# Start addresses of matmul operands: activation tiles and high weight parts at different 32-byte slots of a 512-byte line

## The chip, the cores and the metric

The kernel runs on one core of a Trainium2 chip. The metric is the device time of one execution in microseconds, lower is better. Activations are 256 tokens wide; all weights come from HBM once per use.

## The reference

One layer of a hybrid decoder (`SEQ` 256, `D_MODEL` 2048, 16 heads of 128, `D_FF` 5632), in float32:

```python
h = rmsnorm(x, g_mix)
proj = h @ w_in                      # q, k, v of 16 heads, then three gates
o_a = stick_breaking_attention(...)  # 4 heads
o_b = moba_attention(...)            # 6 heads
o_c = dilated_attention(...)         # 6 heads
merged = (gates[:, :, 0] * (flat(o_a) @ w_branch[:ea])
          + gates[:, :, 1] * (flat(o_b) @ w_branch[ea:eb])
          + gates[:, :, 2] * (flat(o_c) @ w_branch[eb:]))
x = x + merged @ w_out
h2 = rmsnorm(x, g_ffn)
gu = h2 @ w_gu
x = x + (silu(gu[..., :D_FF]) * gu[..., D_FF:]) @ w_down
```

## The kernel before

Nearly all work is the product of 256 tokens with a weight matrix. Tokens are taken as two halves of 128 (`t`), the depth in pieces of 128 rows (`k`), the output in columns of `NB` = 512. Each factor is kept as two tiles of type float32r, a high part and a low part. `split` (L102) makes them: ScalarE (ACT in the profile) casts the source to the high part (L103), VectorE (DVE) subtracts it from the source and writes the low part (L104). `product` (L157) adds three matmuls into one PSUM bank:

```python
nc.tensor.matmul(ps, ah, wh, start=start, stop=False, **how)   # L159
nc.tensor.matmul(ps, ah, wl, start=False, stop=False, **how)   # L160
nc.tensor.matmul(ps, al, wh, start=False, stop=stop, **how)    # L161
```

The first operand (`ah`, `al`: 128x128 of an activation) is what TensorE (PE) loads beforehand with a LDWEIGHTS (PEld in the profile); the second (`wh`, `wl`: 128x512 of a weight part) is streamed through the array. So in the profile's words the model's weights are streamed and the model's activations are loaded.

Weights: `weights` (L106) and `load` (L275) fetch two depth pieces at a time, 512 KB, with SyncE's (SP) queue into `w_raw` (4 buffers) or, where a sum is wanted first, `g_raw`. `weights` and `parts` (L281) split them into `w_hi` and `w_lo`, five buffers each, all in one pool, `wpool` (L82), at the right end of the memory. `project` (L139) is a plain product. `project_pair` (L315) and `down_pair` (L842) trade some of the products for sums of tiles: VectorE adds quarters of the weights into `u` or `g_raw` (L300, L311), and sums of activations are kept as further pairs of parts.

Activations: `Columns` (L185) holds a pair for the whole depth: `h` for the first projections, `o` for the branch projections, `m` for the output projection. `Chunks` (L235) holds a pair for each 512 rows of depth, and for some of them four more tiles: `h2` for the feed-forward part, `a` for the down projection. `Sums` and `Both` (L209, L265) hold the pairs of sums (`b_shi`, `b_slo` and the like). They are allocated in pools at the left end of the memory (`p1`, `pe`, `h2p`, `pd`), `m` at the right end.

The stages follow one another: first projections with the attention woven in (10 to 552 us of the profiled span), branch projections (to 644), output projection (to 734.5), feed-forward (to 1197), down projection. Attention's own matmuls and the transposes (L181) are fp32. A scheduler orders the instructions of each engine when the program is built; DMAs and a few instructions are kept in the order written. A tile's address follows from the order and the sizes of the allocations in its pool alone.

Of the kernel before, what the change touches and what calls it, by code (L numbers as in the profile page):

```python
# [10 lines left out]
F32 = mybir.dt.float32  # L11
F32R = mybir.dt.float32r
# [6 lines left out]
P = 128  # L19
D = 2048  # L20
S = 256
# [8 lines left out]
NB = 512  # L30
# [25 lines left out]
def hybrid_block(ctx: ExitStack, tc: tile.TileContext, x, g_mix, w_in, q_gain, k_gain, w_branch, w_out,  # L56
# [5 lines left out]
    consts = ctx.enter_context(tc.tile_pool(name="consts", bufs=1))  # L62
# [4 lines left out]
    att = pat.enter_context(tc.tile_pool(name="att", bufs=1, space=PSUM))  # L67
    dram = ctx.enter_context(tc.tile_pool(name="dram", bufs=1, space=DRAM))

    gmix = consts.tile([KT, P], F32, name="gmix")  # L70
    nc.scalar.dma_start(gmix, g_mix[0].rearrange("(k p) -> k p", p=P))
    nc.scalar.preload_act_table_set("natural_log_exp_and_others")
# [5 lines left out]
    def pool(stack, name, side, bufs=1):  # L78
        return stack.enter_context(tc.tile_pool(name=name, bufs=bufs, side=side, reuse_waits="tile"))

    h2_stack, ph1, pm, pgx = ExitStack(), ExitStack(), ExitStack(), ExitStack()
    wpool = pool(ctx, "wpool", "right", 5)  # L82
    scratch = pool(ctx, "scratch", "right", 12)
    gx = pool(pgx, "gx", "right", 2)
# [17 lines left out]
    def split(hi, lo, src):  # L102
        nc.scalar.copy(hi, src)  # L103
        nc.vector.tensor_sub(lo, src, hi.bitcast(F32))  # L104

    def weights(w, row0, nk, col0, fine):  # L106

        for c in range(0, nk, 2):
            raw = wpool.tile([P, 2, NB], F32, name="w_raw", bufs=4)
            hi = wpool.tile([P, 2, NB], F32R, name="w_hi")  # L110
            lo = wpool.tile([P, 2, NB], F32R, name="w_lo")
            src = w[row0 + c * P: row0 + (c + 2) * P, col0: col0 + NB].rearrange("(k p) n -> p k n", p=P)
            if fine and c < 4:
                for k in range(2):
                    nc.scalar.dma_start(raw[:, k, :], src[:, k, :])
                    split(hi[:, k, :], lo[:, k, :], raw[:, k, :])
                    yield c + k, hi[:, k, :], lo[:, k, :]
                continue
            nc.sync.dma_start(raw, src)
            split(hi, lo, raw)  # L120
            for k in range(2):
                yield c + k, hi[:, k, :], lo[:, k, :]
# [4 lines left out]
    def advance(queue):  # L127
        while queue:
            try:
                next(queue[0])  # L130
                return
            except StopIteration:
                queue.pop(0)
# [5 lines left out]
    def project(acts, k0, w, row0, nk, col0, fine=False, last=1):  # L139


        ps = banks()
        held = []
        for k, w_hi, w_lo in weights(w, row0, nk, col0, fine):
            if k:
                advance(stages)
            if k % 2 == 0 and k:
                advance(slow_stages)
            held.append((k, w_hi, w_lo))
            if k < nk - last or k == nk - 1:  # L150
                for t in range(NT):
                    for kk, hi, lo in held:
                        product(ps[t], *acts.plain(t, k0 + kk), hi, lo, kk == 0, kk == nk - 1)
                held = []
        return ps
# [26 lines left out]
        return pt  # L182


    class Columns:  # L185


        def __init__(self, pl, name, nk):
            self.hi, self.lo = (pl.tile([P, nk, S], F32R, name=f"{name}_{n}") for n in ("hi", "lo"))

        def put(self, c, t, src):
            k, q = slice(4 * c, 4 * c + 4), slice(t * P, (t + 1) * P)
# [16 lines left out]
    class Sums:  # L209
# [6 lines left out]
                    self.place(pl, c)  # L216

        def place(self, pl, c):
            self.s[c] = [pl.tile([P, 4, S], F32R, name=f"{self.name}_s{n}{c}") for n in ("hi", "lo")]

        def put_sums(self, c, t0, t1, whole=None):
            sums(t0, t1)
# [12 lines left out]
    class Chunks(Sums):  # L235
# [9 lines left out]
        def place(self, pl, c):  # L245
            if c in self.wc:
                super().place(pl, c)
                self.t[c] = [[pl.tile(sh, F32R, name=f"{self.name}_{t}{n}{c}") for n in ("hi", "lo")]
                             for t, sh in enumerate(([P, 4, P], [P, 2, P]))]
            else:  # L250
                self.t[c] = [pl.tile([P, 4, S], F32R, name=f"{self.name}_{n}{c}") for n in ("hi", "lo")]

        def put(self, c, t, src):
            if c in self.wc:
# [24 lines left out]
        return raw  # L279

    def parts(src):  # L281
        hi = wpool.tile([P, 2, NB], F32R, name="w_hi")
        lo = wpool.tile([P, 2, NB], F32R, name="w_lo")
        split(hi, lo, src)
        advance(stages)
        split_count[0] += 1
        if split_count[0] % 2:
            advance(slow_stages)
        return hi, lo
# [15 lines left out]
    def begin_pair(acts, w, colA, colB):  # L305

        b11, b12 = (quarter(acts, w, 0, col0) for col0 in (colA, colB))
        p11 = [parts(b) for b in b11]
        u = [gx.tile([P, 2, NB], F32, name="u") for _ in acts.wc]
        for a, b, d in zip(b11, b12, u):  # L310
            nc.vector.tensor_add(d, a, b)  # L311
        b21 = quarter(acts, w, 1, colA)
        return p11, b12, u, b21, [parts(b) for b in b21]

    def project_pair(acts, w, colA, colB, begun=None, nxt=None):  # L315
# [7 lines left out]
        def form(ps, f, srcs, start, stop, split=False):  # L323
            for i, c in enumerate(acts.wc):
                wh, wl = srcs[i] if split else parts(srcs[i])
                for j in range(2):
                    product(ps, *acts.form(f, c, j), wh[:, j], wl[:, j], start and i + j == 0,
                            stop and i + j == len(acts.wc))
# [417 lines left out]


    pe = pool(ctx, "pe", "left")
    h2 = Chunks(pool(h2_stack, "h2p", "left"), "h", KT // 4, WC)

    def next_h(c, xc):
# [215 lines left out]
```

## Time and profile before

| | |
|---|---|
| median of the runs | 1434.8 us (1433.98 and 1435.62) |
| profiled execution, its own time | 1435.5 us |
| its span | 1433.8 us |
| granted TensorE clock | 0.998 |
| PE busy | 1422.4 us (99%), 6407 matmuls |
| PE weight loads busy | 1173.4 us (82%) |
| VectorE busy | 1195.9 us (83%) |
| ScalarE busy | 880.0 us (61%) |
| DMA | 310.09 MB, mean 216 GB/s |

A matmul's duration in the profile is longer than the distance to the next one, since matmuls overlap; the distance of their starts, the pitch, is what adds up to the span. A row of the view by windows gives the stretch, its length, and for each engine busy time and, in brackets, how many instructions touch the stretch; then the clock, the DMA share and GB/s.

### The profile page before, as it was taken

The page shows a single profiled execution, that of the slowest core. Times are in us where ns is not written, and L with a number is a line of the kernel's source. Part 1 is how long each engine was busy: PE and PEld are TensorE (multiplying, and loading weights), DVE is VectorE, ACT ScalarE, POOL GpSimd, SP SyncE. Part 2 cuts the span into 40 slices and gives each one's busy share as a digit, 9 for nine tenths or more (in the row PEclk, how much of TensorE's full clock was granted, in tenths as well). Part 3 has the DMA queues.
Part 4 walks back from the last instruction along what each step waited for, and adds up shares of the span by engine and source line. Part 5 has one row for each costly group of instructions (what it writes and reads, how often), then busy time and mean ns, then how long its engine had stood idle before and what let it go on. Part 6 is the DMA issues. An engine that isn't in the chain of part 4 may idle for free. (4 is left out here: it accounts for less than half of the span.)

```text
span 1433.8 us, 17776 instructions
## 1 busy us (share of the span) xinstructions
PE 1422.4 (99%) x6407; PEld 1173.4 (82%) x6407; DVE 1195.9 (83%) x1263; ACT 880.0 (61%) x1131; POOL 72.6 (5%) x133
## 2 busy tenths in 40 slices
PE   9999999999999999999999999999999999999998
PEld 7888888888888888888887888888888888888887
DVE  7798797966999887776689999999999998886775
ACT  6567866766766665444556666666666666654453
POOL 1000000000000002100100000000000010100000
PEclk9999999999999999999999999999999999999999
DMA  8763647465656768866686667566666766767553
GB/s 267 253 224 113 233 117 250 118 219 179 219 194 247 245 203 282 287 218 216 217 298 222 216 209 262 201 228 231 222 203 200 243 205 223 262 229 242 188 170 97
DMA packets 154472, 310.09 MB, mean 216 GB/s; under 512 B 10672, under 2 KB 12288, under 8 KB 154384
## 3 DMA queue, kind: packets, MB, share of 16 engines
q1 hardware_dynamic: 142624, 274.24, 57.1%
q0 software_dynamic: 10000, 32.62, 6.9%
q10 hardware_dynamic: 1760, 2.11, 0.4%
q8 instruction: 50, 0.82, 0.2%
q14 instruction: 38, 0.31, 0.1%
HBM read 292.65 MB, written 16.27 MB: 215 GB/s over the span
## 5 line engine op out<-in xcount | busy, mean ns | idle before, releaser
L104 DVE TENSOR_TENSOR w_lo<-w_raw,w_hi 128x1024 fp32r<-128x1024 f32 (+1 forms) x338 | 408.7, 1215 | 94.6 <-ACT w_hi L103 90.7
L103 ACT CAST w_hi<-w_raw 128x1024 fp32r<-128x1024 f32 (+1 forms) x338 | 351.5, 1047 | 176.3 <-PE qs L161 65.8
L103 ACT CAST w_hi<-g_raw 128x1024 fp32r<-128x1024 f32 x184 | 192.5, 1053 | 122.5 <-PE ps L161 39.5
L104 DVE TENSOR_TENSOR w_lo<-g_raw,w_hi 128x1024 fp32r<-128x1024 f32 x184 | 219.6, 1222 | 35.6 <-ACT w_hi L103 34.9
L103 ACT CAST w_hi<-u 128x1024 fp32r<-128x1024 f32 x138 | 145.0, 1053 | 134.9 <-DVE u L300 64.8
L104 DVE TENSOR_TENSOR w_lo<-u,w_hi 128x1024 fp32r<-128x1024 f32 x138 | 166.5, 1222 | 36.2 <-ACT w_hi L103 34.8
L160 PE MATMUL ps<-w_lo,h_hi 128*128 128x512 f32 x368 | 144.1, 392 | 0.0
L161 PE MATMUL ps<-w_hi,h_lo 128*128 128x512 f32 x368 | 143.0, 390 | 0.0
L159 PE MATMUL ps<-w_hi,h_hi 128*128 128x512 f32 x368 | 140.4, 393 | 0.0
L160 PE MATMUL qs<-w_lo,h_hi 128*128 128x512 f32 x332 | 129.9, 391 | 0.8 <-DVE w_lo L104 0.8
L161 PE MATMUL qs<-w_hi,h_lo 128*128 128x512 f32 x332 | 129.4, 390 | 0.0
L159 PE MATMUL qs<-w_hi,h_hi 128*128 128x512 f32 x332 | 126.2, 391 | 0.0
L300 DVE TENSOR_TENSOR u<-u,g_raw 128x1024 f32<-128x1024 f32 x80 | 94.4, 1219 | 0.0
L159 PEld LDWEIGHTS ps<-w_hi,h_hi 128*128 128x128 f32 x368 | 69.2, 188 | 15.1 <-ACT h_hi L103 1.1
L161 PEld LDWEIGHTS ps<-w_hi,h_lo 128*128 128x128 f32 x368 | 69.3, 188 | 14.2
L160 PEld LDWEIGHTS ps<-w_lo,h_hi 128*128 128x128 f32 x368 | 69.3, 188 | 14.0
L160 PEld LDWEIGHTS qs<-w_lo,h_hi 128*128 128x128 f32 x332 | 62.3, 188 | 13.9 <-DVE w_lo L104 1.2
L161 PEld LDWEIGHTS qs<-w_hi,h_lo 128*128 128x128 f32 x332 | 62.4, 188 | 12.8
L159 PEld LDWEIGHTS qs<-w_hi,h_hi 128*128 128x128 f32 x332 | 62.3, 188 | 12.7
L311 DVE TENSOR_TENSOR u<-g_raw 128x1024 f32<-128x1024 f32 x40 | 48.8, 1221 | 23.3 <-DMA g_raw<-in_w_in 18.0
L159 PE MATMUL v<-w_hi,h_hi 128*128 128x512 f32 x120 | 47.5, 396 | 0.2 <-ACT w_hi L103 0.2
L160 PE MATMUL v<-w_lo,h_hi 128*128 128x512 f32 x120 | 47.1, 392 | 0.0
(376 smaller groups left out, 2915.4 us busy)
## 6 DMA issues: line engine op xcount, KB each, us to landing
w_raw<-in_w_in SPq DMA_DIRECT2D x118, 512.0 KB, 4.7
g_raw<-in_w_gu SPq DMA_DIRECT2D x88, 512.0 KB, 5.3
w_raw<-in_w_gu SPq DMA_DIRECT2D x88, 512.0 KB, 6.4
g_raw<-in_w_in SPq DMA_DIRECT2D x72, 512.0 KB, 5.8
w_raw<-in_w_down SPq DMA_DIRECT2D x64, 512.0 KB, 4.6
w_raw<-in_w_branch SPq DMA_DIRECT2D x32, 512.0 KB, 5.0
w_raw<-in_w_out SPq DMA_DIRECT2D x32, 512.0 KB, 4.7
g_raw<-in_w_down SPq DMA_DIRECT2D x24, 512.0 KB, 5.2
```

What stands on the lines that cost most here:

```text
L103: nc.scalar.copy(hi, src)
L104: nc.vector.tensor_sub(lo, src, hi.bitcast(F32))
L159: nc.tensor.matmul(ps, ah, wh, start=start, stop=False, **how)
L160: nc.tensor.matmul(ps, ah, wl, start=False, stop=False, **how)
L161: nc.tensor.matmul(ps, al, wh, start=False, stop=stop, **how)
L300: tc.keep_in_program_order(nc.vector.tensor_add(d, d, a))
L311: nc.vector.tensor_add(d, a, b)
```

## The change

Tiles that nothing reads or writes are allocated to push others to new addresses, and each `w_hi` buffer is 64 bytes longer than its contents. A line is here 512 bytes of a partition, a slot 32 bytes of it, 0 to 15. As built, the tiles begin at these slots:

| tiles | before | after |
|---|---|---|
| `w_raw` | 15 | 6 |
| `w_hi`, five buffers | 15 | 6, 8, 10, 12, 14 |
| `w_lo`, five buffers | 15 | 0 |
| `h_hi`, `h_lo` of the first projections | 7 | 2, 4 |
| sums of `h` (`b_shi`, `b_slo`, two of each) | 7 | 6, 8, 10, 12 |
| `o_hi`, `o_lo` | 7 | 14, 0 |
| `m_hi`, `m_lo` | 15 | 4, 6 |
| `h2` and `a`, all parts and sums | 7 | odd slots, 1 to 15 |

What a matmul reads inside a tile begins at a multiple of 512 bytes from the tile's start, so these are the slots of the operands too. The diff:

```diff
--- before.py
+++ after.py
@@ -67,6 +67,7 @@
     att = pat.enter_context(tc.tile_pool(name="att", bufs=1, space=PSUM))
     dram = ctx.enter_context(tc.tile_pool(name="dram", bufs=1, space=DRAM))
 
+    consts.tile([P, 72], F32, name="fill")
     gmix = consts.tile([KT, P], F32, name="gmix")
     nc.scalar.dma_start(gmix, g_mix[0].rearrange("(k p) -> k p", p=P))
     nc.scalar.preload_act_table_set("natural_log_exp_and_others")
@@ -79,6 +80,8 @@
         return stack.enter_context(tc.tile_pool(name=name, bufs=bufs, side=side, reuse_waits="tile"))
 
     h2_stack, ph1, pm, pgx = ExitStack(), ExitStack(), ExitStack(), ExitStack()
+    LINE = 512
+    pool(ctx, "rim", "right").tile([P, (LINE - 32) // 4], F32, name="rim")
     wpool = pool(ctx, "wpool", "right", 5)
     scratch = pool(ctx, "scratch", "right", 12)
     gx = pool(pgx, "gx", "right", 2)
@@ -103,11 +106,15 @@
         nc.scalar.copy(hi, src)
         nc.vector.tensor_sub(lo, src, hi.bitcast(F32))
 
+    def w_hi_tile():
+
+        return wpool.tile([P, 2 * NB + LINE // 32], F32R, name="w_hi")[:, :2 * NB].rearrange("p (k n) -> p k n", k=2)
+
     def weights(w, row0, nk, col0, fine):
 
         for c in range(0, nk, 2):
             raw = wpool.tile([P, 2, NB], F32, name="w_raw", bufs=4)
-            hi = wpool.tile([P, 2, NB], F32R, name="w_hi")
+            hi = w_hi_tile()
             lo = wpool.tile([P, 2, NB], F32R, name="w_lo")
             src = w[row0 + c * P: row0 + (c + 2) * P, col0: col0 + NB].rearrange("(k p) n -> p k n", p=P)
             if fine and c < 4:
@@ -182,11 +189,19 @@
         return pt
 
 
+    fills = [0]
+
+    def own(pl, shape, name):
+
+        fills[0] += 1
+        pl.tile([P, LINE // 32], F32, name=f"fill{fills[0]}")
+        return pl.tile(shape, F32R, name=name)
+
     class Columns:
 
 
         def __init__(self, pl, name, nk):
-            self.hi, self.lo = (pl.tile([P, nk, S], F32R, name=f"{name}_{n}") for n in ("hi", "lo"))
+            self.hi, self.lo = (own(pl, [P, nk, S], f"{name}_{n}") for n in ("hi", "lo"))
 
         def put(self, c, t, src):
             k, q = slice(4 * c, 4 * c + 4), slice(t * P, (t + 1) * P)
@@ -216,7 +231,7 @@
                     self.place(pl, c)
 
         def place(self, pl, c):
-            self.s[c] = [pl.tile([P, 4, S], F32R, name=f"{self.name}_s{n}{c}") for n in ("hi", "lo")]
+            self.s[c] = [own(pl, [P, 4, S], f"{self.name}_s{n}{c}") for n in ("hi", "lo")]
 
         def put_sums(self, c, t0, t1, whole=None):
             sums(t0, t1)
@@ -245,10 +260,10 @@
         def place(self, pl, c):
             if c in self.wc:
                 super().place(pl, c)
-                self.t[c] = [[pl.tile(sh, F32R, name=f"{self.name}_{t}{n}{c}") for n in ("hi", "lo")]
+                self.t[c] = [[own(pl, sh, f"{self.name}_{t}{n}{c}") for n in ("hi", "lo")]
                              for t, sh in enumerate(([P, 4, P], [P, 2, P]))]
             else:
-                self.t[c] = [pl.tile([P, 4, S], F32R, name=f"{self.name}_{n}{c}") for n in ("hi", "lo")]
+                self.t[c] = [own(pl, [P, 4, S], f"{self.name}_{n}{c}") for n in ("hi", "lo")]
 
         def put(self, c, t, src):
             if c in self.wc:
@@ -279,7 +294,7 @@
         return raw
 
     def parts(src):
-        hi = wpool.tile([P, 2, NB], F32R, name="w_hi")
+        hi = w_hi_tile()
         lo = wpool.tile([P, 2, NB], F32R, name="w_lo")
         split(hi, lo, src)
         advance(stages)
@@ -746,6 +761,7 @@
 
 
     pe = pool(ctx, "pe", "left")
+    pe.tile([P, LINE // 64], F32, name="fill")
     h2 = Chunks(pool(h2_stack, "h2p", "left"), "h", KT // 4, WC)
 
     def next_h(c, xc):
```

## The prediction

> **What bounds the kernel now.** I read the page first (busy time, groups), then the time by stage, then the starts of single matmuls in two stages that differ in where their tiles begin, and last who waited for whom.
>
> ```profile
> span 1433.8 us, 17776 instructions
> PE 1422.4 (99%) x6407; PEld 1173.4 (82%) x6407; DVE 1195.9 (83%) x1263; ACT 880.0 (61%) x1131; POOL 72.6 (5%) x133
> PE qs L160 <- DVE w_lo L104: 1.4, 3, 0.8
> PE ps L160 <- DVE w_lo L104: 1.1, 2, 0.8
> ```
>
> PE is busy for 1422.4 of 1433.8 us, and the waits of PE for a weight part (the last two lines, from the list of PE's own waits) are 1.4 and 1.1 us in all. So the end is set by how many matmuls PE runs and how far apart they start. The long matmuls come from three lines of `product`:
>
> ```profile
> 0.00:1433.80 1433.80, 748.12 (x1988) 373.12 (x1988) 1.00 0.65 216
> 0.00:1433.80 1433.80, 777.64 (x1988) 373.51 (x1988) 1.00 0.65 216
> 0.00:1433.80 1433.80, 773.62 (x1988) 373.52 (x1988) 1.00 0.65 216
> ```
>
> These are the whole span for L159, L160 and L161 alone (PE busy, PEld busy, clock, DMA share, GB/s): 3 x 1988 = 5964 matmuls of 128x512. L160 is the one that streams a low weight part; the other two stream a high part. The distance of their starts, the pitch, is what the change could touch. Here are the first and last rows of the timeline of PE in 584 to 604 us (branch projections, activations `o`) and 673.5 to 693.5 us (output projection, activations `m`), and the window rows of five stretches without other PE work:
>
> ```profile
> 583.64 0.39 PE L159 MATMUL qs<-w_hi,o_hi 128*128 128x512 f32 x1
> ...
> 603.82 0.39 PE L161 MATMUL qs<-w_hi,o_lo 128*128 128x512 f32 x1
> ...
> 673.12 0.39 PE L160 MATMUL ps<-w_lo,m_hi 128*128 128x512 f32 x1
> ...
> 693.30 0.39 PE L159 MATMUL qs<-w_hi,m_hi 128*128 128x512 f32 x1
> ...
> 490.00:510.00 20.00, 20.00 (x90) 16.53 (x90) 20.00 (x20) 12.82 (x14) 0.00 (x0) 1.00 0.53 190
> 584.00:604.00 20.00, 20.00 (x90) 16.57 (x89) 16.05 (x20) 7.39 (x7) 2.20 (x5) 1.00 0.85 294
> 673.50:693.50 20.00, 20.00 (x90) 16.57 (x89) 13.61 (x18) 10.70 (x15) 2.17 (x4) 1.00 0.72 238
> 1005.00:1025.00 20.00, 20.00 (x90) 16.56 (x89) 19.37 (x19) 12.52 (x14) 0.00 (x0) 1.00 0.58 197
> 1220.00:1240.00 20.00, 20.00 (x90) 16.57 (x89) 17.56 (x21) 11.87 (x14) 1.08 (x2) 1.00 0.67 226
> ```
>
> With 90 matmuls in the answer, both first-to-last distances are 20.18 us over 89 steps: 226.7 ns in the one stage, 226.7 ns in the other. All five stretches hold 90, at a granted clock of 1.00, whether VectorE is busy for 13.61 or 20.00 of the 20 us and whether the DMA share is 0.53 or 0.85. So the pitch does not answer to what the other engines and transfers do, and 5964 x 0.2267 = 1352 us of the span are these matmuls.
>
> **The change part by part.** As built, the changed kernel has the same instructions in the same order on every engine, the same DMAs in each queue, and one wait fewer on VectorE's queue. No work is removed or added: unwritten tiles push others to new addresses. So everything hangs on whether a start address has a price. I count addresses in slots of 32 bytes within a 512-byte line, 0 to 15. Before, every weight part (streamed by PE) begins at slot 15 and every activation (loaded as PE's weights) at slot 7, except `m`, which begins at slot 15 too. After, `w_lo` begins at 0, the five `w_hi` buffers at 6, 8, 10, 12 and 14; of the activations, those of the first projections lie at even slots from 2 to 12, `o` at 14 and 0, `m` at 4 and 6, and those of the feed-forward part and the down projection at odd slots; `w_raw` at 6.
>
> *Streaming against weight load.* The distance in slots between what PE streams and what it loads for the next matmul is 8 in four of the quoted stretches and 0 in that of `m`. If two reads that begin in one slot got in each other's way, the `m` rows would be longer. They are not: 226.7 against 226.7 ns. I therefore cost the new distances at 0 for the sum.
>
> The bounds: below, what the pitch could lose at most. The fp32 matmuls of the attention give a rate:
>
> ```profile
> 120.21 1.02 PE L502 MATMUL att<-qT,kT 128*128 128x256 f32 x4
> 121.07 0.38 PE L504 MATMUL att<-qT,kT 128*128 128x128 f32 x2
> ```
>
> Four passes of 256 columns take 121.07 - 120.21 = 0.86 us, 215 ns each. If L159's matmuls, with twice the columns per pass, had twice the rate and nothing else, their pitch would be 215 ns (an estimate), and 11.7 of the 226.7 ns are of unknown make. All of it gone: 5964 x 11.7 ns = 70 us, 1366 us. Above: nothing in the rows caps a new collision, but the nearest price is the same 11.7 ns once more. The new distances other than 0 and 8 cover 5253 of the 5963 steps of the built layout: 5253 x 11.7 ns = 61 us, 1497 us. I take 0, between these, because the only row that varies a distance shows none.
>
> The Trainium skill (TensorE: Matmul & The Clock Gate, "Back-to-back issue gap") gives a warm gap of N/2.4 + 2.5 ns, 215.8 ns at 512 columns; this trace shows 226.7, so page and trace differ by 10.9 ns. By the page's figure the whole excess would be 5964 x 10.9 = 65 us. The skill's page SBUF — State Buffer ("Who interferes with whom") speaks against any effect of this change: it gives PE two independent read ports, so that a weight load takes nothing from a stream. By that rule the time stays; the equal rows of `o` and `m` agree, the unexplained 10.9 ns do not prove it.
>
> *The split on ACT and VectorE, and the transfers.* Tiles that ACT casts and VectorE subtracts move too.
>
> ```profile
> L104 DVE TENSOR_TENSOR w_lo<-w_raw,w_hi 128x1024 fp32r<-128x1024 f32 x334 | 405.9, 1222 | 91.9 <-ACT w_hi L103 88.0 <-PE qs L160 0.2
> L104 DVE TENSOR_TENSOR h_lo<-sc,h_hi 128x512 fp32r<-128x512 f32 x12 | 8.2, 684 | 0.1
> L103 ACT CAST w_hi<-w_raw 128x1024 fp32r<-128x1024 f32 x334 | 349.2, 1052 | 171.2 <-PE qs L161 65.8 <-PE ps L161 46.4 <-issue 13.4
> L103 ACT CAST h_hi<-sc 128x512 fp32r<-128x512 f32 x12 | 7.3, 616 | 2.1 <-DVE sc L406 2.1
> 800.00:1197.00 397.00, 396.26 (x1782) 327.71 (x1781) 368.64 (x344) 252.89 (x286) 17.27 (x26) 1.00 0.65 221
> ```
>
> `w_lo<-w_raw,w_hi` works on three tiles that all begin at slot 15, `h_lo<-sc,h_hi` on tiles at 7, 15 and 7. From 512 to 1024 elements VectorE adds 538 ns, less than double of 684, so the all-equal case pays no premium per element; ACT adds 436 ns to 616, the same picture. Nothing is there to be won, and I cost it at 0. The cover for a loss is PE: in the feed-forward stage (last row) VectorE is busy 368.64 of 397.00 us, so up to 28 us, 7.7%, hide; beyond that each further per cent costs 3.7 us. DMAs write `w_raw` and the like at new slots; their mean share is at most 0.85 in the stretches above, so some 15% more time per packet lies beside PE, and I cost them at 0 as well; without that cover 1% more in the stretch of share 0.85 would be 0.2 us per 20 us.
>
> The sum, against the profiled execution's own time: 1435.5 us (span 1433.8 and 1.7 around it) + 0 = 1435.5. That execution lies 0.7 above the median of the runs, 1434.8, so the forecast is 1434.8.
>
> **The rivals.**
>
> *A third is aligned (faster).* The unknown 11.7 ns may belong to a stream that does not begin at the line's edge: 2048 bytes from slot 15 touch five lines, from slot 0 four. Then L160's 1988 matmuls lose 11.7 ns, 23 us: 1412. For it: every tile that L159 to L161 stream begins at slot 15, so no row contradicts. Against it: nothing but that no row shows it. If each touched line has a share of the excess instead, the gain is a quarter or less of that, 6 us. In both cases VectorE's reserve of 7.7% covers the faster PE.
>
> *The excess goes for all (faster by over 2%).* It may come from starts that are odd multiples of 32 bytes (slots 15 and 7), or from distances 0 and 8 both being bad. After the change all streams begin at even slots. 1366 us by the sum, with a brake: in the feed-forward stage 1782 matmuls would give back 21 us, to 376, where VectorE's 368.64 is 98%, so some 5 us of waits for `w_lo` (L104) come back: about 1371. For it: the excess is there in every stretch and moves with nothing else, like something fixed by layout. Against it: a fixed cost of this kind of matmul would look the same.
>
> *New collisions (slower).* A weight load starts beside each stream; at distances other than 0 and 8 the two could meet in one slot. Price 11.7 ns on up to 5253 steps: up to 1497, half of it 1466. It decides from 5.5 ns a step on (28.7 us, 2%). For it: in 88% of the steps the distances are new, odd ones in the feed-forward part included. Against it: equal starts, the plainest meeting, cost nothing in `m`.
>
> *VectorE becomes the bound (slower).* A subtraction that reads and writes at three different slots could take 10% more; then 368.64 grows to 405.5, over the stage's 397.00, and about 9 us are added: 1444. It decides the sign from 7.7% on. For it: `w_hi` and `w_lo` part ways in every subtraction. Against it: `h_lo<-sc,h_hi`, with mixed slots, is not dear at 684 ns.
>
> **How the numbers follow.** No effect 0.52; a third aligned 0.14; the excess gone for all 0.12; new collisions 0.16; VectorE 0.06. The likeliest is no effect, 1434.8 us, with a range of its own of 1431 to 1439. For eight times in ten the range takes in the aligned third and the smaller half of the collisions: 1400 to 1460; left out are the large gain (0.12) and the large collisions (about 0.08). A difference of 2%, 28.7 us, is about what a measurement of this kernel can tell from no change. Faster by more than that: 0.12, and 0.04 from an aligned third that is worth more than priced, 0.16. Slower by more: 0.14 of the 0.22 of the two slow cases. Within 2%: 0.70.
>
> **What would show each step.** Right: 90 matmuls in 20 us in the same five stages, first to last 20.18 us, and 1222 and 1052 ns for L104 and L103. A third aligned: steps out of L160 shorter than those out of L159 and L161, 91 to 92 in 20 us. All gone: 94 or 95. Collisions: fewer than 90, and unequal in `m`, `o` and the feed-forward part. VectorE: more than 1222 ns in L104 and long waits of PE for `w_lo`. The forecast is wrong if the pitch leaves 226.7 ns by more than 0.6 ns (4 us) in any long stage.

## The result and the profile after

The changed kernel takes 1460.58 us (1459.95 and 1461.2) against 1434.8 us. It is slower by 25.8 us; the ratio on record is 1.0175, with a 95% interval of 1.0158 to 1.0192. (Here and below the ratios are those on record with the runs; the quotients of the medians lie within 0.0005 of them.) From the page of the changed kernel, span and busy time:

```profile
span 1458.2 us, 17775 instructions
PE 1449.1 (99%) x6407; PEld 1173.2 (80%) x6407; DVE 1197.5 (82%) x1263; ACT 879.2 (60%) x1131; POOL 72.8 (5%) x133
```

The profiled execution took 1459.95 us. PE is busy 26.7 us longer with the same 6407 matmuls, and no other engine moved by more than 1.6 us. Windows of 20 us in the same stages as before (first projections, branch projections, output projection, feed-forward, down projection):

```profile
495.00:515.00 20.00, 20.00 (x88) 16.25 (x87) 19.93 (x20) 13.09 (x14) 0.00 (x0) 1.00 0.56 200
591.50:611.50 20.00, 20.00 (x89) 16.20 (x87) 14.30 (x18) 7.35 (x8) 2.42 (x5) 1.00 0.84 283
683.00:703.00 20.00, 20.00 (x88) 16.21 (x87) 13.41 (x17) 10.54 (x15) 2.17 (x4) 1.00 0.67 227
1015.00:1035.00 20.00, 20.00 (x88) 16.10 (x87) 18.95 (x19) 12.39 (x14) 0.00 (x0) 1.00 0.69 234
1235.00:1255.00 20.00, 20.00 (x88) 16.15 (x87) 20.00 (x23) 12.74 (x14) 1.65 (x3) 1.00 0.66 225
```

Where five windows held 90 matmuls each, four now hold 88 and one 89, at the same granted clock of 1.00. The first and last matmul of the second and third window, from the timeline of PE:

```profile
591.13 0.40 PE L168 MATMUL qs<-w_hi,o_lo 128*128 128x512 f32 x1
...
611.50 0.39 PE L166 MATMUL qs<-w_hi,o_hi 128*128 128x512 f32 x1
...
682.64 0.40 PE L167 MATMUL ps<-w_lo,m_hi 128*128 128x512 f32 x1
...
702.84 0.39 PE L167 MATMUL qs<-w_lo,m_hi 128*128 128x512 f32 x1
```

From the first to the last are 20.37 us over 88 steps in the one and 20.20 us over 87 steps in the other: a pitch of 231.5 and 232.2 ns, where it was 226.7 in both. Single steps are uneven now: in a few microseconds of the output projection one finds

```profile
707.65 0.39 PE L166 MATMUL qs<-w_hi,m_hi 128*128 128x512 f32 x1
707.87 0.40 PE L167 MATMUL qs<-w_lo,m_hi 128*128 128x512 f32 x1
708.11 0.40 PE L168 MATMUL qs<-w_hi,m_lo 128*128 128x512 f32 x1
```

steps of 0.22 and 0.24 us. Over the whole trace the 5809 steps from one of the three lines to the next that are shorter than 245 ns have a mean of 232.06 ns; before, 5798 such steps had 227.01. That is 5.05 ns more, 29.3 us in 5800 steps. The longer steps (stalls, and the return from fp32 work) hold 9.2 us beyond the pitch in place of 13.6, which gives 4.4 us back: 24.9 us in all, against 24.4 us by which the span grew. ScalarE and VectorE have no part in it, as the groups of the split show:

```profile
L107 DVE TENSOR_TENSOR w_lo<-w_raw,w_hi 128x1024 fp32r<-128x1024 f32 x334 | 406.5, 1223 | 96.3 <-ACT w_hi L106 94.4
L106 ACT CAST w_hi<-w_raw 128x1024 fp32r<-128x1024 f32 x334 | 348.9, 1050 | 179.1 <-PE qs L168 75.1 <-PE ps L168 55.6 <-issue 11.0
```

1223 and 1050 ns, against 1222 and 1052.

### The profile page after: what moved, and what is told of

It is laid out like the page before. It is cut to its first block, busy times and chain, and to the rows that moved or that the text cites. A ratio compares the mean times of both kernels' runs of the same rounds, so it can differ in the third digit from the quotient of the medians.

```text
span 1458.2 us, 17775 instructions
## 1 busy us (share of the span) xinstructions
PE 1449.1 (99%) x6407; PEld 1173.2 (80%) x6407; DVE 1197.5 (82%) x1263; ACT 879.2 (60%) x1131; POOL 72.8 (5%) x133
## 4 chain that ended last, share of the span: by engine, by line
PE 82%; DVE 2%; DMA 1%; issue 1%; ACT 0%; SPq 0%; DVEq 0%
PE qs L167 9%; PE qs L168 9%; PE qs L166 9%; PE ps L167 9%; PE ps L166 9%; PE ps L168 9%; PE z L167 4%; PE z L166 4%; PE z L168 4%; PE v L166 3%; PE v L168 3%; PE v L167 3%; PE tr L168 1%; PE tr L167 1%; PE tr L166 1%; DVE w_lo L107 1%
## 5 line engine op out<-in xcount | busy, mean ns | idle before, releaser
L106 ACT CAST w_hi<-g_raw 128x1024 fp32r<-128x1024 f32 x184 | 192.2, 1050 | 132.5 <-PE ps L168 44.7
L107 DVE TENSOR_TENSOR w_lo<-u,w_hi 128x1024 fp32r<-128x1024 f32 x138 | 166.7, 1223 | 40.4 <-ACT w_hi L106 40.0
L167 PE MATMUL ps<-w_lo,h_hi 128*128 128x512 f32 x368 | 145.4, 395 | 0.0
L168 PE MATMUL ps<-w_hi,h_lo 128*128 128x512 f32 x368 | 144.3, 394 | 0.0
L166 PE MATMUL ps<-w_hi,h_hi 128*128 128x512 f32 x368 | 141.6, 396 | 0.0
L167 PE MATMUL qs<-w_lo,h_hi 128*128 128x512 f32 x332 | 131.5, 396 | 0.6 <-DVE w_lo L107 0.6
L168 PE MATMUL qs<-w_hi,h_lo 128*128 128x512 f32 x332 | 130.8, 394 | 0.0
L166 PE MATMUL qs<-w_hi,h_hi 128*128 128x512 f32 x332 | 127.6, 395 | 0.0
L166 PEld LDWEIGHTS ps<-w_hi,h_hi 128*128 128x128 f32 x368 | 69.1, 188 | 16.5 <-ACT h_hi L106 0.9
L168 PEld LDWEIGHTS ps<-w_hi,h_lo 128*128 128x128 f32 x368 | 69.1, 188 | 16.0
L167 PEld LDWEIGHTS ps<-w_lo,h_hi 128*128 128x128 f32 x368 | 69.1, 188 | 15.5
L167 PEld LDWEIGHTS qs<-w_lo,h_hi 128*128 128x128 f32 x332 | 62.3, 188 | 15.2 <-DVE w_lo L107 1.1
L166 PEld LDWEIGHTS qs<-w_hi,h_hi 128*128 128x128 f32 x332 | 62.4, 188 | 14.4
L168 PEld LDWEIGHTS qs<-w_hi,h_lo 128*128 128x128 f32 x332 | 62.3, 188 | 14.4
L326 DVE TENSOR_TENSOR u<-g_raw 128x1024 f32<-128x1024 f32 x40 | 48.9, 1223 | 23.6 <-DMA g_raw<-in_w_in 17.2
L166 PE MATMUL v<-w_hi,h_hi 128*128 128x512 f32 x120 | 48.0, 400 | 0.1
L167 PE MATMUL v<-w_lo,h_hi 128*128 128x512 f32 x120 | 47.6, 397 | 0.0
```

## The experiments

"Slot" and "distance" are used as in the prediction: 32-byte slots, and the slot of a load less that of the stream. The three kernels whose names begin with map leave the layer out and run groups of 60 matmuls with chosen starts; in the others the layer is whole.

**A map of distances.** The kernel `map_slots` has two tiles, one to stream from and one to load from, and steps through starts:

```diff
+    for w in range(16):
+        segment(f"hold_{L[15]}{L[w]}", [(stream(15), loads(w))])
+    for w in range(16):
+        segment(f"hold_a{L[w]}", [(stream(0), loads(w))])
...
+        segment(f"stream_{L[m]}", [(hi, ah), (lo, ah), (hi, al)])
...
```

The lines left out (`...`) choose the operands of the triples and add the other groups.

> Matmuls of the same kind alone, 60 to a group, nothing else running; all of the layer is left out. Groups: streams held at slot 15 and loads held at one of the 16 slots; the same with streams at 0; the product's triple with the high stream at another slot than the low stream; the triple with the second load at another slot than the first; starts off by 1, 2 and 4 elements. Three theories. Change theory (a pitch of 226.7 ns is reached when each matmul starts at the same slots as the one before, and a change of slot costs up to 13 ns): all 32 held groups settle at 226.7 ns after some ten matmuls, and the triples with two slots lie at 229 to 236 ns. Distance theory (a stream and the load beside it collide at some distances): held groups at distance 0 and 8 stay at 226.7 ns and several others lie at 230 to 238 ns. Address theory (even slots are dear): held groups with streams at 0 are dearer than those at 15 whatever the load.

The timeline gives one row for each group (start, length, line, tile, count; the second letter is the load's slot, a for 0):

```profile
241.54 13.94 PE L48 MATMUL hold_aa<-sw,la 128*128 128x512 f32 x60
255.54 14.26 PE L48 MATMUL hold_ab<-sw,la 128*128 128x512 f32 x60
269.86 14.27 PE L48 MATMUL hold_ac<-sw,la 128*128 128x512 f32 x60
284.18 14.32 PE L48 MATMUL hold_ad<-sw,la 128*128 128x512 f32 x60
298.56 14.21 PE L48 MATMUL hold_ae<-sw,la 128*128 128x512 f32 x60
312.83 14.27 PE L48 MATMUL hold_af<-sw,la 128*128 128x512 f32 x60
327.16 14.02 PE L48 MATMUL hold_ag<-sw,la 128*128 128x512 f32 x60
341.24 14.27 PE L48 MATMUL hold_ah<-sw,la 128*128 128x512 f32 x60
355.56 13.90 PE L48 MATMUL hold_ai<-sw,la 128*128 128x512 f32 x60
```

Nothing else runs, and the lengths differ: 13.94 and 13.90 us at slots 0 and 8, 14.32 at slot 3. The first ten or so steps of a group are uneven; the mean of its last 44 steps is its settled pitch:

| distance in slots | 0, 8 | 1, 9 | 2, 10 | 3, 11 | 4, 12 | 5, 13 | 6, 14 | 7, 15 |
|---|---|---|---|---|---|---|---|---|
| pitch, ns, streams at 0 | 226.7 | 233.3 | 233.3 | 234.3 | 232.6 | 233.2 | 228.9 | 233.3 |

With streams at 15 the same list comes out by distance, within 0.4 ns. So the address theory falls (slot 0 is no dearer than 15), and the change theory as stated falls (a held group can be dear). The distance theory stands, with a repeat that it had not stated: 8 slots, 256 bytes. The triples, in which the product's three matmuls alternate, are free only where all slots are equal modulo 8, and otherwise lie at 228.9 to 234.6 ns.

**Pads without steps, and each half of the steps alone.**

```diff
# edge_held: the changed kernel, with
-        return wpool.tile([P, 2 * NB + LINE // 32], F32R, name="w_hi")[...]
+        return wpool.tile([P, 2, NB], F32R, name="w_hi")
-        pl.tile([P, LINE // 32], F32, name=f"fill{fills[0]}")
# acts_stepped: the first two lines alone; high_stepped: the third alone
```

> The changed kernel with its pads but without steps: all weight parts at slot 0, all activations of the projections at 0, those of the feed-forward part and the down projection at 1. Change theory: as before, 1435 us within 3, pitch 226.7 ns in long stretches. Distance theory: distance 0 is free, so the projections are as before, and distance 1 covers the later 640 us, with some 25 of the extra 25.7 us times 0.45, about 1446 us. Address theory: as after, 1455 to 1465 us.

> The changed kernel with its steps for the activations alone; all weight parts at slot 0. Change theory: loads change slot once or twice in each three matmuls, so a good part of the loss stays, 1445 to 1458 us, pitch 229 to 232 ns. Distance theory: the same list of distances as after but fewer, 1445 to 1460 us. Address theory: as after, about 1460 us.

> The changed kernel with its steps for the high weight parts alone; all activations at slots 0 and 1. Change theory: streams change slot twice in each three matmuls, so most of the loss stays, 1448 to 1460 us, pitch 230 to 232 ns. Distance theory: 1445 to 1460 us. Address theory: about 1460 us. If this and the run with stepped activations are both near 1460, the losses do not add, as a cost of change that is paid once a matmul would have it.

Measured: `edge_held` 1451.16 us, ratio 1.0103 (1.0088 to 1.0118); `acts_stepped` 1455.78, 1.0135 (1.012 to 1.0151); `high_stepped` 1461.8, 1.0175 (1.0158 to 1.0192); all against 1436.15 us for the kernel before on that chip. Windows of `edge_held`, in the first, branch and output projections and the feed-forward part:

```profile
490.00:510.00 20.00, 20.00 (x89) 16.54 (x89) 20.00 (x20) 12.39 (x13) 0.00 (x0) 1.00 0.55 190
606.00:626.00 20.00, 20.00 (x90) 16.57 (x89) 14.46 (x19) 7.40 (x8) 2.41 (x5) 1.00 0.79 252
673.00:693.00 20.00, 20.00 (x90) 16.58 (x89) 13.60 (x18) 10.78 (x15) 2.17 (x4) 1.00 0.69 234
1010.00:1030.00 20.00, 20.00 (x87) 16.12 (x87) 18.97 (x18) 11.70 (x13) 0.00 (x0) 1.00 0.56 187
```

At distance 0 (the first three) 89 or 90 matmuls, against 90 before; at distance 1 (the last) 87. The mean steps are 226.8 ns in the long stretches of the projections and 233.3 in the feed-forward part, and the map says 226.7 and 233.3. The change theory (1435 us) and the address theory (1455 to 1465) both miss `edge_held`. For the distance theory I had expected 1446 us from a share of the average loss; distance 1 is dearer than the average. The two halves of the steps lose 19.6 and 25.7 us and both together 25.8: the losses do not add. These two runs do not separate the theories: 1455.78 us lies in the ranges of both the change and the distance theory, and 1461.8 us lies 1.8 us above both.

**Held distances.** If distance decides, a kernel without a single step can be made slower than the changed one. These two are the kernel before with a pad at the left end, which moves every activation but `m`:

```diff
+    consts.tile([P, 24], F32, name="fill")     # held_three: 96 bytes
+    consts.tile([P, 48], F32, name="fill")     # held_six: 192 bytes
```

> The kernel before with 96 bytes of pad, so that every activation but m lies three slots further on; nothing is stepped. Distance theory: pitch 234.3 ns but for m, 5584 steps dearer by 7.6 ns, 42 us, of which a fifth is taken up by waits of PE that disappear, as in the earlier run at distance 1: about 1470 us, slower than the changed kernel with all its steps. Change theory (only a change of slot costs): 1436 us.

> The kernel before with 192 bytes of pad: every activation but m at distance 6. Distance theory: pitch 229.0 ns, 5584 steps dearer by 2.3 ns, 13 us less a fifth: about 1446 us. Change theory: 1436 us.

Measured 1469.83 us, 1.0236 (1.0221 to 1.0252), and 1445.13 us, 1.0062 (1.0047 to 1.0077), against 1435.84. One pad of 96 bytes costs more than the whole change, and both numbers are within 1 us of what the map gave. Windows of `held_three`, the same four stages:

```profile
500.00:520.00 20.00, 20.00 (x87) 16.06 (x86) 19.83 (x20) 12.83 (x14) 0.00 (x0) 1.00 0.55 195
596.70:616.70 20.00, 20.00 (x87) 16.09 (x86) 14.82 (x19) 7.92 (x9) 2.97 (x6) 1.00 0.84 284
688.50:708.50 20.00, 20.00 (x89) 16.52 (x88) 13.70 (x18) 10.95 (x16) 2.17 (x4) 1.00 0.70 234
1030.00:1050.00 20.00, 20.00 (x87) 16.10 (x86) 18.06 (x17) 11.26 (x12) 0.00 (x0) 1.00 0.65 213
```

87 in three stages, 89 in that of `m`, which did not move against its weights.

**Steps of 256 bytes.** The counterpart: starts that change all the time, but by whole repeats.

```diff
# high_stepped, with
-        return wpool.tile([P, 2 * NB + LINE // 32], F32R, name="w_hi")[...]
+        return wpool.tile([P, 2 * NB + LINE // 8], F32R, name="w_hi")[...]
-    pe.tile([P, LINE // 64], F32, name="fill")
```

> The changed kernel with high weight parts in steps of 256 bytes in place of 64 (slots 0 and 8 in turn), low parts and activations at slot 0 (m and w_raw at 8). Distance theory with a repeat of 256 bytes: as before, 1436 us within 3, though starts change all the time. Change theory: near the run with stepped high parts, 1455 to 1462 us.

Measured 1435.42 us, ratio 1.0002 (0.9992 to 1.0011). Four of the five windows of the kernel before hold 90 matmuls again, and the fifth holds 92 because four short fp32 transposes fall into it. Two of the four:

```profile
584.00:604.00 20.00, 20.00 (x90) 16.52 (x89) 15.56 (x20) 7.96 (x8) 2.17 (x4) 1.00 0.86 279
...
1005.00:1025.00 20.00, 20.00 (x90) 16.54 (x90) 19.38 (x19) 12.17 (x13) 0.00 (x0) 1.00 0.55 185
```

So different starts as such cost nothing and bring nothing; among whole slots, what counts is the start modulo 256 bytes.

**A finer map, and other operands.** `map_fine` moves the load in steps of 4 bytes and varies sizes and types:

```diff
+    for e in range(64):
+        segment(f"fine_{L[e // 4]}{L[e % 4]}", s0, la[:, e:e + P])
...
+        segment(f"cols_a{c}", s0, la[:, 0:n], cols=n)
...
+        segment(f"width_a{c}", sw[:, 0:n], la[:, 0:P])
...
+        segment(f"half_{L[d]}", sh[:, 0:NB], lh[:, 16 * d:16 * d + P])
...
+        segment(f"full_{L[d]}", raw[:, 0:NB], raw[:, 1024 + 8 * d:1024 + 8 * d + P], n=30)
```

> Matmuls of one kind alone, 60 to a group; all of the layer is left out. First 64 groups in which the load begins 0, 4, 8 ... 252 bytes after the stream's slot; then fewer loaded columns (128, 96, 64, 32) and fewer streamed ones (512, 384, 256) at distance 0 and at three slots; then two-byte and fp32 operands at distances of 0 to 7 slots. Distance theory (stream and load share something that repeats every 256 bytes): distance 0 gives 226.7 ns, three slots 234.3, and the two groups of the first map that were off by elements fall on the same curve (231.7 ns at 16 bytes less, 236.7 at 4 less). If the extra over half the fp32 pitch (215 ns) is the load's reads, the pitch falls with the loaded columns, to about 218 ns at 32, and fp32, which streams at half the rate, shows no dependence on distance (430 ns). Rival, a fixed cost of this kind of matmul: 226.7 ns at distance 0 with any number of loaded columns. Whether a distance finer than a slot lies under 226.7 ns is open to both.

```profile
868.91 13.90 PE L43 MATMUL fine_pa<-sw,la 128*128 128x512 f32 x60
...
982.44 14.01 PE L43 MATMUL cols_ac<-sw,la 128*64 128x512 f32 x60
...
1067.25 10.68 PE L43 MATMUL width_ab<-sw,la 128*128 128x384 f32 x60
...
1096.22 7.38 PE L43 MATMUL width_dc<-sw,la 128*128 128x256 f32 x60
1103.75 13.11 PE L43 MATMUL half_a<-sh,lh 128*128 128x512 bf16 x60
...
1143.26 13.11 PE L43 MATMUL half_d<-sh,lh 128*128 128x512 bf16 x60
...
1209.09 26.02 PE L43 MATMUL full_a<-raw 128*128 128x512 f32 x60
...
1287.32 26.02 PE L43 MATMUL full_d<-raw 128*128 128x512 f32 x60
```

Of 64 distances none is under 226.66 ns; five reach it within 0.1 (0, 120, 132, 156 and 240 bytes), the rest lie at 228.9 to 237.4. The kernel before therefore already has the best pitch of all the distances tried. Two-byte operands (13.11 us a group at every distance, 215.8 ns settled) and fp32 ones (26.02 us, 429.2 ns a pass of 512 columns) show no dependence at the eight distances tried, 0 to 7 slots. Two expectations missed. Fewer loaded columns did not bring the pitch towards 218 ns: at distance 0 it went up to 230.0, 229.8 and 231.7 ns with 96, 64 and 32, and at three slots it came down from 234.3 to 230.7, 231.5 and 230.5. So the extra over 215 ns is not shown to be the load's reads, nor is it a cost that stays the same for any number of loaded columns; with fewer than 128 of them the two distances differ by 1.6 ns at most. And the earlier groups fit the curve only where the load was off by elements (232.4, 230.7 and 233.3 ns at 4, 8 and 16 bytes in both runs); where the stream was, one of three does (233.3 in both at 8 bytes less) and two do not (236.7 against 233.3 at 4 bytes less, 231.7 against 226.7 at 16 less).

**Which load?** The last run alternates two matmuls, so that either the load beside a stream or the stream's own load matches it:

```diff
+    for x in range(1, 9):
...
+        segment(f"own_{L[x]}", [(stream(0), loads(0)), (stream(x, 1), loads(x, 1))])
...
+        segment(f"next_{L[x]}", [(stream(0), loads(x)), (stream(x, 1), loads(0, 1))])
...
+        segment(f"turn_{L[x]}", [(stream(0), loads(0)), (stream(0, 1), loads(x, 1))])
```

> Matmuls of one kind alone, two in turn; all of the layer is left out. In the groups 'own' each load begins at the slot of its own matmul's stream (0 and x in turn), so the load that runs beside a stream is x slots off; in the groups 'next' each load begins at the slot of the stream that it runs beside, one matmul earlier, so that its own stream is x slots off; in the groups 'turn' streams are held at 0 and loads alternate between 0 and x. Beside-theory (a stream is slowed by the load for the next matmul, by their distance): 'next' stays at 226.7 ns for all x, 'own' lies at 229 to 236 ns for x of 1 to 7, and 'turn' about half as far above 226.7 as 'own'. Own-theory (a matmul's own load and stream have to match): the other way round. Change theory in its last form (any change of slot that is not a multiple of 256 bytes costs, whatever the distance): all three at 229 to 236 ns. All: 226.7 ns at x of 8.

```profile
99.16 14.46 PE L48 MATMUL own_e<-sw,la 128*128 128x512 f32 x60
113.68 14.08 PE L48 MATMUL next_e<-sw,la 128*128 128x512 f32 x60
...
227.15 13.94 PE L48 MATMUL next_i<-sw,la 128*128 128x512 f32 x60
...
283.54 14.20 PE L48 MATMUL turn_e<-sw,la 128*128 128x512 f32 x60
```

Settled, `own` lies at 231.5 to 236.7 ns for x of 1 to 7, `next` at 230.0 to 231.7, `turn` at 230.0 to 233.3, and all three at 226.7 for x of 8. A match with the load beside the stream makes it cheaper than a match with the stream's own load at five of the seven slots, by 1.7 to 6.7 ns, and not at 2 and 6 (231.7 in both at 2, 231.7 against 231.5 at 6). It is free at none, so neither the beside- nor the own-theory holds alone; a change of start by other than 256 bytes costs at least 3.3 ns even where each stream matches the load beside it. Of the three, the last form of the change theory is what stands here. But a mismatch that never changes costs too, as the held groups of the first map and `held_three` show, so what the runs leave is one rule: among whole slots, every start has to agree modulo 256 bytes. What sets the size between 229 and 237 ns, and why 120, 132, 156 and 240 bytes are free as well, is open.

## Why the prediction was wrong

The step that failed is the one headed *Streaming against weight load*. It had one natural trial in the trace, `m` at distance 0 and everything else at 8, found both at 226.7 ns, and priced all new distances at 0. To the chip the two are the same distance: the map repeats every 8 slots. The row that seemed to vary the distance did not vary it, and 14 of the 16 distances had never been seen. The measured price is 5.05 ns on 5800 steps, 29.3 us, for the 0 of the sum.

The rival *new collisions* was the right one in place, sign and order of size: its 88% of steps at new distances got dearer, and the others with them (in the first projections 230.5 ns at distance 8), as in the alternating pairs. Its price of 11.7 ns a step was more than twice the 5.05 ns measured; held distances of whole slots cost 2.3 to 7.6 ns, and the dearest of the 64 fine ones 10.7, so as a bound it stood. I gave it 0.16. Its reason against, that equal starts are the plainest meeting and cost nothing, was the mistake turned into a chance. The range ended at 1460, which cut the rival off below its own middle of 1466; the result lies 0.6 us outside. The chances do not fit together either: 0.14 for slower by more than 28.7 us, which is above 1463, is more than the 0.08 left for collisions above 1460, and VectorE's case was priced at 1444. (Counted from the addresses in the built program, 5264 steps have a new distance and not 5253, which makes 0.1 us of difference.)

Weighting the settled pitches of the map with the distances of the changed kernel's 5963 steps, by the addresses in the built program, gives a mean of 232.0 ns, and 232.06 was measured; for `edge_held` 230.0 against 230.3. For the changed kernel the agreement is partly luck. Sorted by distance, its steps have a mean of 230.8 ns at 0 and 8 (226.7 in the map), 232.1 at 3 and 11 (234.3) and 231.4 at 6 and 14 (228.9): where distances change all the time, cheap ones get dearer and dear ones cheaper, and only the mean comes out. For the two half-stepped kernels the weighting is 1.3 ns too high and 0.6 too low. A held distance is not the whole rule, as the pairs show.

Right: the same matmuls at the same clock; nothing at ACT and VectorE, whose instructions kept their times; transfers without effect; no aligned third (with `w_lo` at slot 0, the steps out of L167, which streams it, have a mean of 232.2 ns, those out of L166 and L168 232.1 and 231.9). The excess for all fell with it: its price of 11.7 ns rested on an estimated pitch of 215 ns, and no start tried brought a float32r matmul of 512 columns under 226.66. VectorE's reserve in the feed-forward stage was never called on. Of the signs listed, "fewer than 90, and unequal" is what the windows show. The waits did one thing that the sum had left out: a slower PE waits less, and 4.4 us came back.

The port rule that I weighed (the Trainium skill, SBUF — State Buffer, "Who interferes with whom") has PE stream and load through independent ports. These runs disagree for float32r: with PE alone at work the pitch goes from 226.7 to 234.3 ns by the load's start alone, and the measurement decides. Whether the loss arises at the ports is not shown. The gap of 215.8 ns for 512 columns, given for an isolated matmul (the Trainium skill, TensorE: Matmul & The Clock Gate, "Back-to-back issue gap"), is what the two-byte operands show, 215.8; float32r does not reach it at any start tried.

## What to carry to other kernels

Where a kernel streams float32r operands 512 columns at a time, allocate so that every tile that PE reads begins at the same place modulo 256 bytes; a stray pad of 96 bytes cost 34 us of 1436 here. Spreading starts over a line was the wrong remedy, and two-byte or fp32 operands showed no need of one. And before a pair of equal rows is taken as proof that something does not matter, ask whether the two cases differ in the unit that the hardware counts in.

## What the runs showed of the hardware

A float32r matmul with 128 loaded columns at matching starts has a cost of 13.3 ns that depends neither on the columns streamed nor, at 512 columns (226.7 ns alone and in the layer), on other engines: 226.66, 173.34 and 120.00 ns for 512, 384 and 256 columns are 53.3 ns for each 128 columns and 13.3 besides. Mismatched starts add up to 10.7 ns (237.4) in held groups of 512 columns; at 384 columns three slots made no difference (173.3 both), and at 256 the mismatched group was shorter, 118.7. Many settled pitches lie at 226.67, 230.0 and 233.33 ns, steps of 3.33 ns, and a group at matching starts needs some ten matmuls to settle; no run here shows why.
